# A float32 encoder trunk on one core: splits, products and weight sums of the adaLN parts placed elsewhere, and wo's early products in another order

## The chip, the core and the metric

The kernel runs on one core of one Trainium2 chip. The core has a matrix engine (TensorE, in the profile PE, with its weight loads as PEld), a vector engine (VectorE, DVE), a scalar engine (ScalarE, ACT), GpSimd (POOL), and SyncE (SP), which here issues most of the DMAs. Each engine works off its own list of instructions in order; semaphores hold an instruction until what it needs is there. The metric is the device time of one execution in microseconds. Before the change it is **1129.53 us**, the median of 3 runs (1127.41 to 1130.43).

## The reference

512 tokens of width 1024 go through two layers. Each has a token mixer (stick-breaking attention in layer 0, a gated token-mixing MLP in layer 1) and a SwiGLU network. Every one of these four sub-layers is wrapped like this:

```python
def ada_modulation(c, w, b):
    m = jax.nn.silu(c) @ w + b
    shift, scale, gate = jnp.split(m, 3, axis=-1)
    return shift[:, None, :], scale[:, None, :], gate[:, None, :]

def swiglu(h, w_gate, w_up, w_down):
    return (jax.nn.silu(h @ w_gate) * (h @ w_up)) @ w_down
...
    shift, scale, gate = ada_modulation(c, ffn_ada_w[i], ffn_ada_b[i])
    h = rms_norm(x, ffn_pre_g[i]) * (1.0 + scale) + shift
    y = swiglu(h, ffn_w_gate[i], ffn_w_up[i], ffn_w_down[i])
    x = x + gate * rms_norm(y, ffn_post_g[i])
```

The mixers have the same frame with their own weights. D_MODEL is 1024, D_FF 2816, everything is float32. What matters here: the adaLN vectors (shift, scale, gate) come from one row vector, silu(c), times a 1024 by 3072 matrix for each of the four sub-layers, 12 MB each.

## The kernel before

**Matmuls.** Tokens lie in four tiles of 128 (NT). A float32 matmul is made of three products of a short float format (`mm3`, L101): high by high, high by low, low by high. `split` (L109) makes the two parts of a value: the high one is a copy on ScalarE, the low one a subtraction on VectorE. In the profile wh and wl are the parts of a weight block, acch and accl those of a half adaLN sum, and as stands for both parts of an activation block. A result gathers in a PSUM bank of 128 by 512. There are six banks with the tag "b" and two with the tag "p" (`bank`, L50).

**Weights** are streamed: `wload` (L124) issues a load of 512 KB into one of two raw buffers, `wemit` (L134) splits it into one of six buffers, `wget` (L203) hands blocks out and stays three blocks ahead. All of these loads go through SP's queue, in the order in which they are written.

**adaLN parts** are made by the class `Bg` (L313), in small steps beside the main matmuls. G, A and B are the gate, the scale and the shift of a sub-layer; A1, B1, G2 and so on carry its number. For each part the eight row blocks of the matrix (rawada, 512 KB each, in two buffers of their own) are multiplied by silu(c) per partition and added to a 128 by 1024 accumulator on VectorE, one `ada_stt` (L306) a block. What remains is the sum over partitions. It is a product with a matrix of ones on TensorE: the accumulator is split in two halves of 512, and each half takes two matmuls (high, low) into a bank of tag "p", in the profile adaps. Then the bank is evacuated: B by a copy on ScalarE, A and G on VectorE, with a norm weight (pre_g or post_g, in the profile g, a load of 512 KB) multiplied in. The generator `run` (L338) yields after each sum, and before the change twice between split and product. `step` (L378) takes it on by so many yields.

**The output projection** `out_proj` (L493) loops over blocks k of its weights and within them over the token tiles; each gives 6 matmuls of 512 columns (two halves by three). For w_down of layer 0 (nk = 22, four of them held back as a tail) it also feeds two `Bg`s: `bg` with A1, B1, G2, two sums a step over the 12 steps k = 0 to 11, and then `bg2` with A2, B2 one sum a step. Token tile 0 gathers in the two "p" banks, which the adaLN products need too. So at `mid` = 13 the partial of tile 0 is copied out (yp), the products use the two banks, and tile 0 takes them again for the rest:

```python
            bg.step(steps)
            if bg2 is not None and mid is not None and k >= mid:
                bg2.step(1)
            if k + 1 == mid:
                yp = slot(F32, "yp")
                for hf in range(2):
                    act.activation(yp[:, hf, :], y[last][hf][:], AF.Copy)
                bg.step(99)
```

**The attention stage** has a generator of filler work (`filler`, L793) that a table of numbers deals out between the parts of a head pair. Its last items are the first four blocks (NEARLY = 4) of the projection wo for the token tiles 3 and 2; tile 3 gathers in the "p" banks, which the products of the last head pair's k and q have used before.

**Order.** In the attention stage all engines keep the order in which the code is written. In w_down and the gMLP stage the compiler's scheduler places instructions by their dependencies, so a step of `Bg` may come out some matmuls later than it is written. `blocks` (L170) makes the derived weight blocks of the SwiGLU stage, in the buffers f13, b21 and f24 (beside e, for silu); between the SwiGLU stages of the two layers these lie idle. `gmlp` (L1303) steps `bg2` on, through the remaining sums of A2 and B2 and their products.

## Time and profile before

| | us |
|---|---|
| runs: median (lowest, highest) | 1129.53 (1127.41, 1130.43) |
| the profiled execution | 1129.13 |
| its span in the trace | 1127.4 |

By stage, from the busy time of each engine in seven stretches of the span:

| stretch, us | stage | PE busy | DVE busy | ACT busy | DMA share |
|---|---|---|---|---|---|
| 0 to 75 | start, qkv begin | 66.42 | 55.98 | 46.44 | 0.80 |
| 75 to 229 | attention, wo | 152.27 of 154 | 123.44 | 100.90 | 0.50 |
| 229 to 505 | SwiGLU 0, gate and up | 276.00 of 276 | 233.86 | 154.56 | 0.44 |
| 505 to 640 | w_down 0 | 132.56 of 135 | 99.97 | 51.82 | 0.70 |
| 640 to 760 | gMLP | 120.00 of 120 | 73.96 | 48.62 | 0.47 |
| 760 to 1000 | SwiGLU 1, gate and up | 240.00 of 240 | 209.59 | 136.01 | 0.38 |
| 1000 to 1127.4 | w_down 1, end | 120.49 | 96.75 | 60.67 | 0.32 |

The granted TensorE clock is 0.99 to 1.00 in every stretch. The table is read by what is missing: TensorE is idle in the first stretch, in the last, and by 1.7 and 2.4 us in the two stretches in which the adaLN parts and wo's early products are made.

In a row of the profile L64 is the helper through which VectorE's and ScalarE's instructions pass, L90 the matmul in `mm`, L98 a transpose, L107 `load`; names are written out<-in without numbers.

### The profile page before, as it was taken

Reading aid. Unit: us, or ns where it says so; the run is one execution under the profiler, and the core shown is the slowest. Engines: PE = TensorE matmul, PEld = TensorE weight load, DVE = VectorE, ACT = ScalarE, POOL = GpSimd, SP = SyncE. Lnnn points to the kernel's source line nnn. Section 1 sums busy time; section 2 is a strip of 40 time slices with the busy share of each in tenths; the row PEclk is TensorE's granted clock in tenths of the full one; section 3 lists DMA queues with packets and bytes.
Section 4 is the critical chain, followed back from the end, with each engine's and each line's share of the span. In section 5 each row is a group of like instructions: output and inputs, shape, how many; then the busy total and the mean of one; then the engine's idle time right before and its main releaser. Section 6 shows DMA issues by size and latency. Waiting matters only on the chain.

```text
span 1127.4 us, 18149 instructions
## 1 busy us (share of the span) xinstructions
PE 1107.7 (98%) x7264; PEld 993.5 (88%) x7264; DVE 893.6 (79%) x1141; ACT 599.0 (53%) x971; POOL 39.7 (4%) x71
## 2 busy tenths in 40 slices
PE   7999999999999999999999999999999999999997
PEld 5788878779999999988878988989999999998895
DVE  7777888759988989687687774659988988788964
ACT  7746767646555555562234534437555555565541
POOL 0220111000000000010000000000000000000000
PEclk9999999999999999999999999999999999999999
DMA  9676445353344444378874583333244444223242
GB/s 363 228 229 164 146 145 164 124 187 131 95 131 150 149 137 129 93 231 262 285 259 158 186 281 89 99 131 131 76 150 149 130 133 133 76 86 105 91 168 75
DMA packets 51298, 176.09 MB, mean 156 GB/s; under 512 B 5643, under 2 KB 6155, under 8 KB 50318
## 3 DMA queue, kind: packets, MB, share of 16 engines
q1 hardware_dynamic: 45166, 153.95, 41.8%
q0 software_dynamic: 6048, 20.98, 5.9%
q8 instruction: 57, 0.93, 0.3%
q14 instruction: 27, 0.22, 0.1%
HBM read 164.43 MB, written 8.39 MB: 153 GB/s over the span
## 4 chain that ended last, share of the span: by engine, by line
PE 84%; DMA 7%; DVE 5%; issue 2%; ACT 1%; SPq 0%; POOL 0%; DVEq 0%; POOLq 0%; ACTq 0%
PE r L90 33%; PE y L90 12%; PE X L90 8%; PE v L90 7%; PE gu L90 6%; DMA rawada<-in_ada 5%; PE pqk L90 5%; PE u L90 4%; PE M L90 2%; PE z L90 1%; PE tw L98 1%; PE av L90 1%; DMA ada<-in_ada0w 1%; PE tp L98 1%; DMA raw<-in_wdown 1%
## 5 line engine op out<-in xcount | busy, mean ns | idle before, releaser
L64 ACT ACTIVATE wh<-raw 128x1024 fp32r<-128x1024 f32 (+1 forms) x112 | 116.8, 1050 | 139.6 <-PE y L90 41.2
L64 DVE TENSOR_TENSOR wl<-raw,wh 128x1024 fp32r<-128x1024 f32 (+1 forms) x112 | 135.0, 1211 | 65.8 <-ACT wh L64 65.5
L90 PE MATMUL r<-Sh,wh 128*128 128x256 f32 x608 | 170.6, 281 | 0.0
L90 PE MATMUL r<-Sl,wh 128*128 128x256 f32 x608 | 170.5, 280 | 0.0
L90 PE MATMUL r<-Sh,wl 128*128 128x256 f32 x608 | 170.3, 280 | 0.0
L90 PE MATMUL y<-wh,as 128*128 128x512 f32 x480 | 153.6, 396 | 0.2 <-DVE G L64 0.2
L64 DVE TENSOR_TENSOR wl<-f,wh 128x1024 fp32r<-128x1024 f32 x76 | 92.8, 1222 | 36.2 <-ACT wh L64 36.2
L64 ACT ACTIVATE wh<-f 128x1024 fp32r<-128x1024 f32 x76 | 80.6, 1061 | 68.4 <-PE r L90 65.1
L90 PEld LDWEIGHTS r<-Sh,wh 128*128 128x128 f32 x608 | 114.8, 189 | 0.2 <-ACT e L64 0.2
L90 PEld LDWEIGHTS r<-Sh,wl 128*128 128x128 f32 x608 | 114.7, 189 | 0.0
L90 PEld LDWEIGHTS r<-Sl,wh 128*128 128x128 f32 x608 | 114.7, 189 | 0.0
L90 PEld LDWEIGHTS y<-wh,as 128*128 128x128 f32 x480 | 90.1, 188 | 21.6 <-DVE G L64 0.7
L90 PE MATMUL y<-wl,as 128*128 128x512 f32 x240 | 94.8, 395 | 0.0
L90 PE MATMUL r<-hTh,wh 128*128 128x256 f32 x304 | 88.9, 293 | 0.0
L90 PE MATMUL r<-hTl,wh 128*128 128x256 f32 x304 | 85.1, 280 | 0.0
L90 PE MATMUL X<-wh,as 128*128 128x512 f32 (+1 forms) x288 | 84.6, 370 | 0.0
L90 PE MATMUL r<-hTh,wl 128*128 128x256 f32 x304 | 80.3, 280 | 0.0
L64 ACT ACTIVATE e<-r 128x256 f32<-128x256 f32 x114 | 43.3, 380 | 52.7 <-PE r L90 52.4
L90 PEld LDWEIGHTS r<-hTh,wh 128*128 128x128 f32 x304 | 57.3, 188 | 4.5 <-DVE gu L64 0.6
L90 PEld LDWEIGHTS X<-wh,as 128*128 128x128 f32 x288 | 52.5, 188 | 9.5
L90 PE MATMUL r<-hTh,b 128*128 128x256 f32 x304 | 60.8, 282 | 0.0
L64 ACT ACTIVATE wh<-rawx 128x1024 fp32r<-128x1024 f32 x38 | 40.3, 1062 | 36.8 <-PE r L90 31.1
(233 smaller groups left out, 2811.8 us busy)
## 6 DMA issues: line engine op xcount, KB each, us to landing
rawada<-in_ada SPq DMA_DIRECT2D x56, 512.0 KB, 5.0
raw<-in_wdown SPq DMA_DIRECT2D x44, 512.0 KB, 4.2
rawy<-in_wy SPq DMA_DIRECT2D x38, 512.0 KB, 3.7
rawx<-in_wx SPq DMA_DIRECT2D x38, 512.0 KB, 4.6
rawada<-in_ada POOLq DMA_DIRECT2D x24, 512.0 KB, 4.3
raw<-in_wqk SPq DMA_DIRECT2D x16, 512.0 KB, 3.8
ada<-in_ada0w SPq DMA_DIRECT2D x7, 1026.0 KB, 10.9
raw<-in_wgu SPq DMA_DIRECT2D x12, 512.0 KB, 3.6
```

The costliest lines, as they stand in the source:

```text
L64: b = f(*a, **k)
L90: b = nc.tensor.matmul(o, l, r, start=start, stop=stop, skip_group_check=True)
L98: last_tp[0] = nc.tensor.transpose(o, i, ident)
```

## The change

It has two parts.

1. In `filler` the loops over halves and blocks change places: half 0 of a token tile takes all four blocks of wo before half 1 begins.
2. `Bg` gets a flag `hold`, set for A1, B1, G2 in w_down of layer 0 and for A2, B2. With it, an accumulator is split right behind its last sum, into buffers that the SwiGLU's weight sums leave idle (`store`); the products need no split any more and come one half (two matmuls) a yield, so with two yields a step A, B and G take k = 12, 13 and 14. `out_proj` holds back tile 0's products of k = 13 and 14 (`put`) and does them at k = 15 together with those of k = 15; the sums of A2 begin at `mid + 2` instead of `mid`.

```diff
@@ class Bg
-        def __init__(self, *parts, slots=False, queue=nc.sync):
-            self.slots = slots
+        def __init__(self, *parts, slots=False, hold=False, queue=nc.sync):
+            self.slots, self.hold = slots, hold
...
         def run(self):
-            for name, at, s, part in self.parts:
+            for n, (name, at, s, part) in enumerate(self.parts):
...
                     ada_stt(acc, raw, k)
+                    if k == KD - 1 and self.hold:
+                        held[name, at] = self.store(n)
+                        for b, (h, l) in enumerate(zip(*held[name, at])):
+                            split(h, l, acc[:, b * 512 : (b + 1) * 512])
                     if not self.slots:
                         yield
...
                 for b in range(2):
                     c = slice(b * 512, (b + 1) * 512)
-                    h = adas.tile([P, 512], F32R, tag="acch", name=nm("acch"))
-                    l = adas.tile([P, 512], F32R, tag="accl", name=nm("accl"))
-                    split(h[:], l[:], acc[:, c])
-                    yield
-                    yield
+                    if self.hold:
+                        h, l = [t[b] for t in held[name, at]]
+                    else:
+                        h = adas.tile([P, 512], F32R, tag="acch", name=nm("acch"))[:]
+                        l = adas.tile([P, 512], F32R, tag="accl", name=nm("accl"))[:]
+                        split(h, l, acc[:, c])
+                        yield
+                        yield
                     ps = self.bank()
...
                         dve.tensor_tensor(acc[:, c], ps[:], g[:, c], ALU.mult)
+                    if self.hold:
+                        yield
+
+        def store(self, n):
+
+            fp = fwork["pool"]
+            if n == 0:
+                t = [fp.tile([P, 2, 512], F32R, tag="f13", name=nm("acc")) for _ in range(2)]
+                return [[x[:, b, :] for b in range(2)] for x in t]
+            if n == 1:
+                return [
+                    [fp.tile([P, 512], F32R, tag=f"b21{i}", name=nm("acc"))[:] for _ in range(2)]
+                    for i in range(2)
+                ]
+            t = fp.tile([P, 2, 512], F32R, tag="f24", bufs=1, name=nm("acc"))
+            return [
+                [t[:, b, :] for b in range(2)],
+                [
+                    fp.tile([P, 768], F32R, tag="e", name=nm("acc"))[:, :512] for _ in range(2)
+                ],
+            ]
@@ out_proj
+        put = []
         for k in range(nk - J):
             a = get_act(k)
             w = pre["w"][k] if k < npre else wget(wkey(k))
+            put.append((k, a, w))
             for tt in range(NT):
-                if k >= npre or tt not in pre["y"]:
+                if mid is not None and tt == last and k >= mid:
+                    if k >= mid + 2:
+                        for j in put:
+                            step(j[0], tt, *j[1:])
+                elif k >= npre or tt not in pre["y"]:
                     step(k, tt, a, w)
-            bg.step(steps)
-            if bg2 is not None and mid is not None and k >= mid:
+            if mid is None or k + 1 < mid or k >= mid + 2:
+                put = []
+            if bg2 is not None and mid is not None and k >= mid + 2:
                 bg2.step(1)
             if k + 1 == mid:
+                put = []
                 yp = slot(F32, "yp")
                 for hf in range(2):
                     act.activation(yp[:, hf, :], y[last][hf][:], AF.Copy)
-                bg.step(99)
+            bg.step(steps)
         bg.step(99)
@@ filler
-                for k, w in enumerate(early["w"]):
-                    for hf in range(2):
+                for hf in range(2):
+                    for k, w in enumerate(early["w"]):
@@ the calls
-    bg2 = Bg("A2", "B2")
+    bg2 = Bg("A2", "B2", hold=True)
     f0.run(
-        Bg("G1", slots=True), Bg("A1", "B1", "G2"), bg2, 2, hT2,
+        Bg("G1", slots=True), Bg("A1", "B1", "G2", hold=True), bg2, 2, hT2,
```

How the instructions move, at three places. In the rows below numbers behind a name tell buffers apart.

The first is TensorE in the attention stage, at the start of tile 3's early products: y_1806 and y_1810 are its halves 0 and 1, wh_1616/wl_1617 are the weights of k = 1, 1708/1709 of k = 2, 1802/1803 of k = 3 (the three rows of k = 0 stand ahead). A row with - is only in the kernel before, one with + only in the changed one:

```order
 L90 MATMUL y_1806<-wh_1616,o_1142 128x512
-L90 MATMUL y_1810<-wh_1616,o_1142 128x512
-L90 MATMUL y_1810<-wl_1617,o_1142 128x512
-L90 MATMUL y_1810<-wh_1616,o_1142 128x512
+L90 MATMUL y_1806<-wh_1708,o_1311 128x512
+L90 MATMUL y_1806<-wl_1709,o_1311 128x512
+L90 MATMUL y_1806<-wh_1708,o_1311 128x512
+L90 MATMUL y_1806<-wh_1802,o_1473 128x512
+L90 MATMUL y_1806<-wl_1803,o_1473 128x512
+L90 MATMUL y_1806<-wh_1802,o_1473 128x512
 L90 MATMUL z_532<-k_1770,q_1685 128x128
```

In the kernel before the 12 matmuls ahead of z take k = 0 and 1 for both halves, and now k = 0 to 3 for half 0 alone; half 1 opens its bank behind z.

The second place is the end of the sums of G2 in w_down of layer 0, on ScalarE and on SP. acc_5670 holds the high parts of G2's sum (G_5546), wh_5728 is the split of w_down's block 16, yp the copy of tile 0's partial. ScalarE in the changed kernel:

```order
L64 ACTIVATE wh_5682<-raw_5680 128x1024
L64 ACTIVATE acc_5670<-G_5546 128x512 x2
L64 ACTIVATE wh_5728<-raw_5726 128x1024
L64 ACTIVATE wh_5763<-raw_5761 128x1024
L64 ACTIVATE yp_5710<-y_5180 128x512
L64 ACTIVATE yp_5710<-y_5184 128x512
L64 ACTIVATE as_5723<-act_4044 128x512
```

SP in the changed kernel; raw_5798 is block 18 of w_down, g_5713 the norm weight for A1's evacuation, A_5842 the bias row of A2, and rawada are row blocks for sums:

```order
L107 DMA rawada_5847<-in_ada 128x1024
L107 DMA raw_5798<-in_wdown 128x1024
L107 DMA g_5713<-in_pre_g 128x1024
L107 DMA g_5785<-in_post_g 128x1024
L107 DMA A_5842<-in_adab 1x1024
L107 DMA raw_5853<-in_wdown 128x1024
```

SP in the kernel before, where g_5689 is the same norm weight:

```order
L107 DMA rawada_5493<-in_ada 128x1024
L107 DMA g_5689<-in_pre_g 128x1024
L107 DMA rawada_5496<-in_ada 128x1024
L107 DMA rawada_5535<-in_ada 128x1024
L107 DMA raw_5583<-in_wdown 128x1024
```

On ScalarE the split of G2 now stands ahead of the weight splits of blocks 16 and 17. On SP the load of g has gone from the midst of G2's row blocks to behind the load of block 18.

The third place is VectorE where G2 is evacuated. In the kernel before, with G_5532 for G2 and A_5779 for the accumulator of A2:

```order
L64 SCALAR_TENSOR_TENSOR A_5779<-rawada_5820,sc,A_5779 128x1024
L64 TENSOR_TENSOR G_5532<-adaps_5732,g_5726 128x512
L64 TENSOR_TENSOR accl_5737<-G_5532,acch_5736 128x512
L64 SCALAR_TENSOR_TENSOR A_5779<-rawada_5856,sc,A_5779 128x1024
L64 TENSOR_TENSOR G_5532<-adaps_5740,g_5726 128x512
```

In the changed kernel, with A_5212 for A1, G_5546 for G2 and A_5842 for A2:

```order
L64 SCALAR_TENSOR_TENSOR A_5212<-adaps_5715,g_5713 128x512
L64 SCALAR_TENSOR_TENSOR A_5212<-adaps_5719,g_5713 128x512
L64 TENSOR_TENSOR wl_5801<-raw_5798,wh_5800 128x1024
L64 SCALAR_TENSOR_TENSOR A_5842<-rawada_5845,sc,A_5842 128x1024
L64 TENSOR_TENSOR as_5943<-act_4798,as_5943 128x512
L64 SCALAR_TENSOR_TENSOR A_5842<-rawada_5847,sc,A_5842 128x1024
L64 TENSOR_TENSOR as_5946<-act_5049,as_5946 128x512
L64 TENSOR_TENSOR as_5949<-act_5049,as_5949 128x512
L64 SCALAR_TENSOR_TENSOR A_5842<-rawada_5883,sc,A_5842 128x1024
L64 SCALAR_TENSOR_TENSOR A_5842<-rawada_5919,sc,A_5842 128x1024
L64 TENSOR_TENSOR G_5546<-adaps_5787,g_5785 128x512
L64 TENSOR_TENSOR G_5546<-adaps_5791,g_5785 128x512
```

Before, one sum of A2 stands between the evacuations of G2's halves and one ahead of them; now four stand between A1's evacuations and G2's first, together with a weight split (wl_5801). Behind G2's first evacuation TensorE opens tile 0's bank again, in both kernels.

More of the change, by code (lines that the diff above doesn't have):

```diff
@@ L309, in ada_stt @@
         )
-    ada = {}
+    ada, held = {}, {}
     class Bg:
-        def __init__(self, *parts, slots=False, queue=nc.sync):
-            self.slots = slots
+        def __init__(self, *parts, slots=False, hold=False, queue=nc.sync):
+            self.slots, self.hold = slots, hold
             self.queue = queue
@@ L362, in run @@
                     c = slice(b * 512, (b + 1) * 512)
-                    h = adas.tile([P, 512], F32R, tag="acch", name=nm("acch"))
-                    l = adas.tile([P, 512], F32R, tag="accl", name=nm("accl"))
-                    split(h[:], l[:], acc[:, c])
-                    yield
-                    yield
+                    if self.hold:
[6 more added lines that the diff above has]
+                        yield
                     ps = self.bank()
-                    mm(ps[:], ones_r, h[:], True, False, last_tp[0])
-                    mm(ps[:], ones_r, l[:], False, True)
+                    mm(ps[:], ones_r, h, True, False, last_tp[0])
+                    mm(ps[:], ones_r, l, False, True)
                     if part == 0:
```

## The prediction, made before the changed kernel ran

> **What bounds the kernel now.** I read the page first, then the list of waits, TensorE's timeline at its waits, the chain, and the tile views of what is late.

> ```profile
> PE 1107.7 (98%) x7264; PEld 993.5 (88%) x7264; DVE 893.6 (79%) x1141; ACT 599.0 (53%) x971; POOL 39.7 (4%) x71
> ...
> PE adaps L90 <- ACT acch L64: 2.2, 1, 2.2
> PE y L90 <- DVE k L64: 1.7, 1, 1.7
> PE y L90 <- DVE G L64: 0.2, 1, 0.2
> ```

> TensorE (PE) is busy for 98% of the span, so a change that keeps its matmuls can only gain what PE now waits. Between 30 and 1110 us it has these three waits (total, times, longest). Part one of the change (wo's early products) stands at the second, part two (the adaLN sums in the first w_down projection) at the others. PE's timeline there:

> ```profile
> 563.79 0.39 PE L90 MATMUL adaps<-acch,ones 128*128 128x512 f32 x1
> ...
> 565.40 0.62 PE L90 MATMUL y<-wh,as 128*128 128x512 f32 x2
> 568.23 0.51 PE L90 MATMUL adaps<-acch,ones 128*128 128x512 f32 x1 [2.20 <-ACT acch L64]
> ...
> 580.85 0.50 PE L90 MATMUL y<-wh,as 128*128 128x512 f32 x1 [0.24 <-DVE G L64]
> ```

> In brackets: the idle time and what ended it. The most that can be gained is 1.73 + 2.20 + 0.24 = 4.2 us, 0.37% of the profiled execution's 1129.13 us (its span is 1127.4; the median of the runs shown, 1129.53, is 0.4 higher). A difference under 0.3% (3.4 us) can hardly be told from none. The first row also gives the pace: seven matmuls of 512 columns start between 563.79 and 565.40, 0.23 us each. The chain says why PE stood still:

> ```profile
> 560.38 6.11 DMA raw<-in_wdown
> ...
> 566.60 1.06 ACT wh L64
> 567.65 0.53 ACT acch L64
> ...
> 568.23 0.51 PE adaps L90
> ...
> 573.13 5.68 DMA rawada<-in_ada
> ...
> 578.90 1.28 DVE A L64
> 580.19 0.61 DVE G L64
> ...
> 580.85 19.17 PE y L90 x81
> ```

> The split of a sum (acch, on ScalarE, ACT) stood behind a weight split (wh) that waited for its load. Later G's evacuation on VectorE (DVE) stood behind a sum of A2 that waited for its load. The second is the pattern to watch: an in-order engine holds an evacuation that PE wants, behind an instruction that waits for a transfer.

> **Part one, wo's early products.** Token tile 3's half 0 now takes k = 0 to 3 before half 1 opens its bank.

> ```profile
> 198.81 2.33 DVE L64 TENSOR_TENSOR_SCAN ga<-ga,tri 128x512 f32<-128x512 f32 x2
> 200.03 0.48 PE L90 MATMUL y<-wh,o 128*128 128x512 f32 x1
> 200.94 1.06 ACT L64 ACTIVATE wh<-raw 128x1024 fp32r<-128x1024 f32 x1
> 201.16 1.39 DVE L64 TENSOR_TENSOR k<-pqk,k 64x512 fp32r<-64x512 f32 x2
> 202.58 0.69 DVE L64 TENSOR_TENSOR o<-av,o 128x512 fp32r<-128x512 f32 x1
> 202.70 0.47 PE L90 MATMUL y<-wh,o 128*128 128x512 f32 x1 [1.73 <-DVE k L64]
> 203.19 1.22 DVE L64 TENSOR_TENSOR wl<-raw,wh 128x1024 fp32r<-128x1024 f32 x1
> 204.88 0.22 PE L90 MATMUL z<-k,q 128*128 128x128 f32 x1
> ```

> Before, the fourth of these 12 matmuls waits until DVE has emptied the bank (k ends at 202.55). After, nine run from 200.03 to about 202.2, and the tenth needs k = 3's weights. Their high part is there (200.94 + 1.06 = 202.0). Their low part (wl) comes behind k and o on a DVE that has no gap from 198.81 on: 203.19 + 1.22 = 204.41. The eleventh so starts at about 204.5, the twelfth 0.34 later as the second one behind such a wait (200.03 to 200.34 would be 0.31), and z at 205.1 against 204.88. **One wait takes the other's place: +0.2 us** (bounds 0 and +0.4), not −1.73.

> **Part two, the sums in w_down 0.** Each sum is split as soon as it is complete, the six products run two a step at k = 12, 13, 14, and the fresh banks of token tile 0 open at k = 15 instead of 13. The acch wait of 2.20 goes. Six ACT and six DVE splits are moved, not added; the sums of A2 start two steps later, and with them their loads on SP's queue. What is late next is G's evacuation, by a chain that the rows price one by one:

> ```profile
> 557.93 1.28 DVE L64 SCALAR_TENSOR_TENSOR G<-rawada,sc,G 128x1024 f32<-128x1024 f32 x1 [1.48 <-DMA rawada<-in_ada]
> 559.13 1.22 DVE L64 TENSOR_TENSOR wl<-raw,wh 128x1024 fp32r<-128x1024 f32 x1
> ...
> 560.38 0.33 SPq L107 DMA_DIRECT2D raw<-in_wdown  x1
> 560.76 0.42 SPq L107 DMA_DIRECT2D g<-in_post_g  x1
> 560.82 1.07 ACT L64 ACTIVATE yp<-y 128x512 f32<-128x512 f32 x2
> ...
> 566.06 0.68 DVE L64 SCALAR_TENSOR_TENSOR A<-adaps,g 128x512 f32<-128x512 f32 x1
> 573.62 1.29 DVE L64 TENSOR_TENSOR as<-act,as 128x512 fp32r<-128x512 f32 x2
> ...
>   DMA rawada<-in_ada: 15.6, 15
> ...
> DMA to landing us min/median/max: 3.6/4.6/5.7
> ...
> DMA to landing us min/median/max: 4.2/5.2/7.4
> ...
> DMA to landing us min/median/max: 7.4/7.4/7.4
> ```

> The last four rows are of the tile views from 520 on: DVE's wait for rawada (15.6 us in 15 waits: the sums are paced by their loads), and the time from issue to landing of rawada, of w_down's raw and of g.

> 1. The last sum of G ends at 559.2. Three inserted pairs of low splits (0.6 each) stand between sums that wait for loads anyway; I let half a microsecond through: 559.8 (bounds 558.9 and 561.0).
> 2. G's split on ACT, two halves, 1.07 like the pair yp: 560.9. It stands ahead of the wh of w_down's block 16, which ran at 559.86 before.
> 3. That wh 1.06: 561.9. Its wl 1.22: 563.1. This frees a raw buffer, and only now SP can issue block 18's raw, with the load of **g** (pre_g, for A's evacuation) queued behind it, 0.38 later: 563.5. (Behind that stand the other g, A2's bias and the next raw.)
> 4. g lands. The one g on record took 7.4, raw's median is 5.2, the shortest transfer of this size 3.6. I take 6.3, midway between raw's median and the g: 569.8 (bounds 3.6 and 7.4).
> 5. A's two evacuations, 1.29: 571.1. Only behind them come a wl (1.1 net of overlap: 572.2), the first two sums of A2 with an "as" of 0.6 between (1.2 + 0.6 + 1.2): 575.2.
> 6. The two sums free the buffers of two more loads of A2, and both sums that use those stand before G's evacuation on DVE. The second is issued at 575.2. I take the 5.68 that the chain shows for the same load at the same place (bounds 3.6 and 5.7): 580.9.
> 7. That sum 1.28, G's evacuation 0.6: 582.8. PE opens the bank at 582.9.

> PE gets there early. The new order has 54 matmuls between the first product (563.79) and this one: 563.79 + 54 × 0.235 = 576.5, with 0.235 from the 81 matmuls in 19.17 us. So PE loses some 6.4 us in all, the greater part, about 5, in one wait on G. Waits before it (for yp's bank, for A's evacuation) are swallowed: the bank opens at 582.9 whether PE waits once or thrice. Before, PE resumes at 580.85 with the 62nd matmul; after, this place in the count is seven further on, at 582.9 + 0.34 + 6 × 0.235 = 584.65. **+3.8 us**; all behind it is the same number of matmuls, and PE has no wait to give it back to.

> With the bounds: all loads at 3.6 and step 1 unchanged end the chain 5.4 earlier, at 577.5, and the step at −1.6. With 561.0 and a g of 7.4 the step is +5.8 to +6.

> The rest of the move I cost at nothing beside this. The deferred products are the same in number. They hold the weights of blocks 13 and 14 two steps longer, so the loads of the last blocks (19 to 21) come later, but PE wants those only in the tail, after 580.85 + 19.17 = 600, some 20 us behind A2's first sums; without that cover each late load would cost its own 4 to 5 us. POOL's clearing of A2's accumulator and its bias load move along and are short of the path by step 4's wait. In the gMLP stage the products of A2 and B2 follow at once, without the two empty steps:

> ```profile
> 667.00 2.61 DVE L64 SCALAR_TENSOR_TENSOR B<-rawada,sc,B 128x1024 f32<-128x1024 f32 x2 [1.02 <-DMA rawada<-in_ada]
> ...
> 671.54 0.40 PE L90 MATMUL adaps<-acch,ones 128*128 128x512 f32 x1
> ```

> The sums end at 669.6 and the first product of B2 is due some 16 matmuls behind the 671.54, at 675.3; A2's evacuation, behind one wh and one wl, is through at about 673.7. I take 0 (bound +1).

> Sum: 1129.13 + 0.2 + 3.8 = **1133.1 us**.

> [...]

> **Rivals.** (a) *The loads are fast, and nothing changes.* The decisive point is the sum of the two loads in steps 4 and 6: at 12.0 − 3.8 = 8.2 us or less (3.6 + 4.6, for one) the change is not slower. For it: 3.6 and 4.6 are on record, and the new order moves A2's loads away. Against it: g, at its old place in this queue, took 7.4, and rawada in the chain 5.68. Time 1127.7 to 1131, the middle 1129.5; 0.17.

> (b) *The wait costs PE its clock too.* No mid-kernel wait of before exceeds 2.4 us; this one is about 5. At the kernel's start, after idle time, matmuls run slow:

> ```profile
> 2.92 3.78 PE L90 MATMUL sc<-pack,sc 128*128 128x128 f32 x16 [2.92 <-ACT sc L64]
> ...
> 9.04 3.32 PE L98 MATMUL tp<-pack,x 128*128 128x128 f32 x20 [0.25 <-DVE x L64]
> ...
> 192.39 1.03 PE L98 MATMUL tw<-pack,ga 128*128 128x128 f32 x8
> ```

> 16 of 128 columns take 3.78 (0.22 each, by their starts), 8 of 128 later take 1.03 with the tail of the last (0.11 each): half pace. The 20 from 9.04 take 3.32, so some nine of them are slow, until about 11: at most 8.1 us of half pace since 2.92, so at most 4.1 lost. With half of that or all of it the time is 1135.1 to 1137.2. Against it: the waits of 1.73 and 2.20 are followed by full pace at once. 0.22. [...]

> (c) *The change does what it says*, and the three waits go with nothing in their place: 1129.13 − 4.2 = 1124.9. It needs wl of k = 3 two microseconds earlier, and a G that no load of A2 holds; the order speaks against both. 0.04.

> **How the numbers follow.** Forecast 0.57, (a) 0.17, (b) 0.22, (c) 0.04. Slower by over 0.3% (above 1132.9): a little over half of the forecast's chance and all but little of (b), together 0.56. Faster by over 0.3% (below 1126.1): 0.04. Within: 0.40. The range leaves out (c), the lower half of (a) and the upper third of (b), together 0.19: 1129.4 to 1136.6.

> **What would show it.** PE's timeline at 202.4 to 204.5 has a wait of about 2 us, named wl, where k stood. At 576 to 583 it has waits that sum to 6 us, the longest on DVE's G, and the acch wait is gone. DVE idles for g until about 570 and for rawada until about 581. If the matmuls behind that wait start 0.43 apart for a while, (b) is right. The forecast is wrong if g or the last rawada lands in under 4.5 us, or if A's evacuation does not stand behind g; then PE opens the bank before 580.

## The result and the profile after

The changed kernel takes **1134.3 us** (median of 6 runs, 1130.09 to 1135.81) against 1129.32 before: a ratio of 1.0038, 95% interval 1.0022 to 1.0055. It is slower by 0.38%, or 4.3 us by the ratio. The profiled execution took 1132.64 us, with a span of 1130.9 against 1127.4.

The page of the changed kernel, busy time of each engine, and the list of what TensorE waited for (total, times, longest):

```profile
PE 1110.6 (98%) x7264; PEld 996.0 (88%) x7264; DVE 893.3 (79%) x1141; ACT 598.4 (53%) x971; POOL 39.8 (4%) x71
...
PE y L90 <- DVE G L64: 2.9, 1, 2.9
PE y L90 <- DVE wl L64: 1.9, 1, 1.9
PE r L90 <- DVE gu L64: 0.3, 1, 0.3
```

Both parts did what the diff says: the waits on k, on acch and the small one on G are gone. In their place stand a wait on wl at wo's early products and one on G in w_down. In sum the waits are little longer: 5.1 us against 4.1. The larger share is in the first row. PE's busy time has grown by 2.9 us (1107.7 to 1110.6) with the same 7264 instructions. The timeline of PE shows where, first at wo's early products and then in w_down:

```profile
204.44 0.50 PE L90 MATMUL y<-wl,o 128*128 128x512 f32 x1 [1.87 <-DVE wl L64]
...
205.01 0.22 PE L90 MATMUL z<-k,q 128*128 128x128 f32 x1
...
206.27 0.63 PE L90 MATMUL y<-wh,o 128*128 128x512 f32 x1
206.70 0.63 PE L90 MATMUL y<-wl,o 128*128 128x512 f32 x1
...
577.97 0.40 PE L90 MATMUL y<-wh,as 128*128 128x512 f32 x1
581.22 0.62 PE L90 MATMUL y<-wh,as 128*128 128x512 f32 x1 [2.85 <-DVE G L64]
581.64 0.63 PE L90 MATMUL y<-wl,as 128*128 128x512 f32 x1
582.07 1.05 PE L90 MATMUL y<-wh,as 128*128 128x512 f32 x2
...
585.21 0.39 PE L90 MATMUL y<-wl,as 128*128 128x512 f32 x1
585.44 0.63 PE L90 MATMUL y<-wh,as 128*128 128x512 f32 x2
```

Matmuls of 512 columns start 0.43 apart at 206.27 and 206.70, and again from 581.22 on, where 0.23 is the usual pace (585.21 to 585.44). TensorE ran at **half pace** for 3.4 us at each of the two waits, and each stretch cost about 1.5 us, by an estimate from the 2.9 above. The granted TensorE clock (the column behind POOL busy) says the same when it is asked for narrow stretches of the changed kernel:

```profile
core 0: us, PE busy (x) PEld busy (x) DVE busy (x) ACT busy (x) POOL busy (x), PEclk, DMA share, GB/s
202.57:205.98 3.41, 1.54 (x10) 1.45 (x11) 3.41 (x4) 1.07 (x2) 0.00 (x0) 1.00 0.82 272
205.98:209.40 3.42, 3.42 (x11) 2.73 (x11) 2.48 (x3) 1.00 (x2) 0.00 (x0) 0.50 0.80 273
581.45:584.86 3.41, 3.41 (x9) 2.61 (x9) 1.60 (x2) 0.80 (x1) 0.00 (x0) 0.50 0.71 221
```

In the profile of before there is no half pace in mid-kernel: its granted clock is 1.00 in each stretch of 40 us from 30 to 1110. The chain of the changed kernel, from the sums to the reopened bank:

```profile
563.14 1.06 ACT wh L64
564.20 0.97 ACT yp L64 x2
565.18 0.52 ACT as L64
...
565.73 3.13 DVE as L64 x6
...
569.35 0.99 DVE A L64 x2
...
570.54 1.21 DVE wl L64
571.76 1.21 DVE A L64
...
572.98 4.89 DMA rawada<-in_ada
...
577.96 1.30 DVE A L64
...
580.48 0.70 DVE G L64
...
581.22 23.99 PE y L90 x95
```

The second half of it is the one forecast: evacuation of A, a weight split, sums of A2, a load for the next sums, these sums, and only then G's evacuation.

### The profile page after: what moved, and what is told of

The parts are those of the page before. It is cut to its first block, busy times and chain, and to the rows that moved or that the text cites. A ratio compares the mean times of both kernels' runs of the same rounds, so it can differ in the third digit from the quotient of the medians.

```text
span 1130.9 us, 18147 instructions
## 1 busy us (share of the span) xinstructions
PE 1110.6 (98%) x7264; PEld 996.0 (88%) x7264; DVE 893.3 (79%) x1141; ACT 598.4 (53%) x971; POOL 39.8 (4%) x71
## 4 chain that ended last, share of the span: by engine, by line
PE 82%; DVE 7%; DMA 7%; issue 2%; ACT 1%; SPq 0%; POOL 0%; DVEq 0%; ACTq 0%; POOLq 0%
PE r L90 31%; PE y L90 12%; PE X L90 8%; PE v L90 7%; PE gu L90 6%; PE pqk L90 5%; PE u L90 4%; DMA rawada<-in_ada 4%; PE M L90 2%; DVE wl L64 2%; PE z L90 1%; DMA raw<-in_wdown 1%; PE tw L98 1%; DMA ada<-in_ada0w 1%; PE av L90 1%
## 5 line engine op out<-in xcount | busy, mean ns | idle before, releaser
L64 DVE TENSOR_TENSOR wl<-raw,wh 128x1024 fp32r<-128x1024 f32 (+1 forms) x112 | 135.0, 1211 | 67.6 <-ACT wh L64 67.3
L64 ACT ACTIVATE wh<-raw 128x1024 fp32r<-128x1024 f32 (+1 forms) x112 | 116.8, 1050 | 120.8 <-PE y L90 34.7
L90 PE MATMUL r<-Sh,wh 128*128 128x256 f32 x608 | 170.5, 280 | 0.0
L90 PE MATMUL r<-Sl,wh 128*128 128x256 f32 x608 | 170.5, 280 | 0.0
L90 PE MATMUL r<-Sh,wl 128*128 128x256 f32 x608 | 170.3, 280 | 0.0
L90 PE MATMUL y<-wh,as 128*128 128x512 f32 x480 | 154.1, 398 | 2.9 <-DVE G L64 2.9
L64 DVE TENSOR_TENSOR wl<-f,wh 128x1024 fp32r<-128x1024 f32 x76 | 92.8, 1221 | 36.1 <-ACT wh L64 36.1
L64 ACT ACTIVATE wh<-f 128x1024 fp32r<-128x1024 f32 x76 | 80.6, 1061 | 68.8 <-PE r L90 65.3
L90 PEld LDWEIGHTS r<-Sh,wh 128*128 128x128 f32 x608 | 114.8, 189 | 0.2 <-ACT e L64 0.2
L90 PEld LDWEIGHTS r<-Sh,wl 128*128 128x128 f32 x608 | 114.7, 189 | 0.0
L90 PEld LDWEIGHTS r<-Sl,wh 128*128 128x128 f32 x608 | 114.7, 189 | 0.0
L90 PEld LDWEIGHTS y<-wh,as 128*128 128x128 f32 x480 | 90.9, 190 | 24.3 <-DVE G L64 3.3
L90 PE MATMUL y<-wl,as 128*128 128x512 f32 x240 | 95.5, 398 | 0.0
L90 PE MATMUL r<-hTh,wh 128*128 128x256 f32 x304 | 88.8, 293 | 0.3 <-DVE gu L64 0.3
L90 PE MATMUL r<-hTl,wh 128*128 128x256 f32 x304 | 85.1, 280 | 0.0
L90 PE MATMUL X<-wh,as 128*128 128x512 f32 (+1 forms) x288 | 84.7, 370 | 0.0
L90 PE MATMUL r<-hTh,wl 128*128 128x256 f32 x304 | 80.2, 280 | 0.0
L64 ACT ACTIVATE e<-r 128x256 f32<-128x256 f32 x114 | 43.5, 381 | 52.7 <-PE r L90 52.4
L90 PEld LDWEIGHTS r<-hTh,wh 128*128 128x128 f32 x304 | 57.2, 188 | 4.9 <-DVE gu L64 1.3
L90 PEld LDWEIGHTS X<-wh,as 128*128 128x128 f32 x288 | 52.5, 188 | 9.6
L90 PE MATMUL r<-hTh,b 128*128 128x256 f32 x304 | 60.8, 282 | 0.0
L64 ACT ACTIVATE wh<-rawx 128x1024 fp32r<-128x1024 f32 x38 | 40.3, 1061 | 36.8 <-PE r L90 31.0
```

The source lines that it names most:

```text
L64: b = f(*a, **k)
L90: b = nc.tensor.matmul(o, l, r, start=start, stop=stop, skip_group_check=True)
```

## The experiments

Two theories were put against each other. **Theory 1:** the change swaps waits for waits of the same length, and the surplus is half pace behind them. **Theory 2, the forecast's:** the chain over A2's sums makes TensorE wait longer, and the pace plays no part. Times are medians; ratios are to the kernel before on the same chip, whose median was 1129.88 (35 runs) beside the first four, 1129.52 (29) beside the next four and 1130.52 (23) beside the last three.

| run | kernel | us | ratio, 95% interval |
|---|---|---|---|
| e1 | part one alone | 1132.98 | 1.0014 (0.9999 to 1.0029) |
| e2 | part two alone | 1133.24 | 1.0028 (1.0012 to 1.0043) |
| e3 | changed, pads of zeros in both waits | 1132.98 | 1.0022 (1.0010 to 1.0033) |
| e4 | changed, A2's sums behind G's evacuation | 1128.19 | 0.9984 (0.9970 to 0.9998) |
| e5 | changed, once more | 1134.68 | 1.0033 (1.0019 to 1.0048) |
| e6 | as e3, tile 1's matmuls ahead of the pads | 1130.78 | 1.0014 (1.0003 to 1.0024) |
| e7 | before, another order of wo's early products | 1127.46 | 0.9987 (0.9975 to 0.9998) |
| e8 | e4 and e7 together | 1126.46 | 0.9967 (0.9955 to 0.9979) |
| e9 | before, with pads | 1131.15 | 1.0012 (0.9996 to 1.0027) |
| e10 | e8 once more | 1125.73 | 0.9951 (0.9931 to 0.9970) |
| e11 | part two alone, A2's sums behind G's evacuation | 1128.30 | 0.9974 (0.9963 to 0.9986) |

### e1 and e2: each part alone

e1 is the kernel before with the two loops exchanged, e2 the changed kernel with the loops as before:

```diff
-                for k, w in enumerate(early["w"]):
-                    for hf in range(2):
+                for hf in range(2):
+                    for k, w in enumerate(early["w"]):
```

> Part one alone on the kernel before. Theory 1 (the change swaps waits for waits of the same length, and its surplus is TensorE at half pace after them, as the profile of the changed kernel shows at 206.3 to 209.0 and at 581.2 to 584.6): the wait of 1.73 us on k is replaced by one of about 1.87 on wl, z starts 0.1 to 0.2 us later, and in some executions a stretch of half pace follows that loses about 1.6 us, so the median lies 0 to 1.8 us above the kernel before. Theory 2 (the forecast: the waits themselves are longer and the pace plays no part): +0.2 us, with no more spread than before.

> Part two alone: the changed kernel with the loops of wo's early products as before. Theory 1: TensorE waits 2.5 to 3.5 us on G at about 579, in place of 2.20 + 0.24 before, and a half-pace stretch behind it loses 1.6: +1.5 to +3 us. Theory 2: the wait on G is about 5 us long, with full pace behind it: +3.8 us. If the chain that ends in G keeps its absolute time, TensorE comes to it 1.7 us earlier than in the changed kernel and the wait is that much longer, so the sum is near that of the changed kernel (+3.5) even without part one.

e1 is 1.6 us slower by the ratio (−0.1 to +3.3), which is not clear of zero. Its runs fall into two groups: 7 of 12 lie above 1132 us, against 7 of 35 for the kernel before. The granted clock on record for each run goes with this: its mean over the run is 0.993 to 0.996 in those seven, and 0.996 to 0.999 in the five others. VectorE's last sum ahead of wo's early products in its profile, the waits of TensorE, and what follows the first:

```profile
197.81 1.28 DVE L64 SCALAR_TENSOR_TENSOR B<-rawada,sc,B 128x1024 f32<-128x1024 f32 x1 [1.68 <-DMA rawada<-in_ada]
...
PE adaps L90 <- ACT acch L64: 2.8, 1, 2.8
PE y L90 <- DVE wl L64: 2.6, 1, 2.6
...
207.81 0.63 PE L90 MATMUL y<-wh,o 128*128 128x512 f32 x1
208.24 0.63 PE L90 MATMUL y<-wl,o 128*128 128x512 f32 x1
```

The wait on wl was longer than forecast here, 2.63 us: VectorE had come late, by a sum of B that waited 1.68 for its load ahead of the scan (0.90 in the profile of before). Half pace follows, 0.43 from start to start, and here it lasts longer: at least from 205.25 to 210.38, 5.1 us against 3.4. So part one, meant for a wait of 1.73, swaps it for one that is as long or longer.

e2 gives +0.28%, the larger part of the change's +0.38% (+0.33% when it was run again, e5). G's evacuation starts at 580.0 there and at 580.5 in the changed kernel, although TensorE came to its first product 1.3 us earlier (564.40 against 565.73). In these two profiles the chain keeps its time, and what TensorE loses ahead of it is swallowed by the wait. The times do not show this: the parts sum to +0.42%, and with the intervals that is not told apart from the whole.

### e3 and e6: TensorE kept busy in the waits

Matmuls with a stationary matrix of zeros add nothing to a bank but occupy TensorE (22 of them take 5.30 us in e3). The two places in e3:

```diff
...
+                        if (tt, hf, k) == (3, 0, 3):
+                            for _ in range(8):
+                                mm(y[0][:], zeros_r, early["w"][0][0][:, 0, c], False, False)
...
+                        if k == mid + 2:
+                            for _ in range(22):
+                                mm(y[3][1][:], zeros_r, put[0][2][0][:, 0, 0:512], False, False)
```

> The changed kernel with matmuls that add zeros to a bank (8 ahead of k = 3 in tile 3's half 0, 22 ahead of tile 0's new banks in w_down), so that TensorE is busy while it waits; at 0.233 us they take 1.9 and 5.1 us, about what the waits take with part one's half pace gone. Theory 1: the half-pace stretches go (-3.2 us in the profile), what is left is the exchange of waits, and pads that outlast the wait cost up to 1 us: 1129.5 to 1131.5, with a small spread. Theory 2: the waits set the time and the pads change nothing: 1133 to 1135.

In e3 the longest wait in mid-kernel is 0.3 us and the matmuls behind the second pads start 0.23 to 0.24 apart (from 581.23 on), and yet the time is that of e2 (+0.22% against +0.28%). The timeline of e3 shows a flaw of the experiment: the six matmuls of tile 1 that fill the wait in the changed kernel (1.4 us) had slipped behind the pads. e6 puts them ahead, with 14 pads.

> As the first padded kernel, but with tile 1's six matmuls of k = 15 ahead of the pads, where the changed kernel has them, and 14 pads in place of 22. Theory 2: G's evacuation starts at 580 to 581 as in the first padded kernel, and with full pace behind it the later part of the kernel is 1.4 us earlier than there: 1131 to 1132.3, which is 1.3 to 2.5 above the kernel before, all of it the chain. Theory 1: without half pace the kernel is level with the one before, 1129 to 1130.3.

PE in e6 at the second wait:

```profile
576.72 0.39 PE L90 MATMUL y<-wh,as 128*128 128x512 f32 x1
576.95 3.44 PE L90 MATMUL y<-wh,zeros 128*128 128x512 f32 x14
580.22 0.39 PE L90 MATMUL y<-wh,as 128*128 128x512 f32 x1
580.45 0.39 PE L90 MATMUL y<-wl,as 128*128 128x512 f32 x1
```

VectorE in e6, where G is evacuated:

```profile
579.13 1.28 DVE L64 TENSOR_TENSOR G<-adaps,g 128x512 f32<-128x512 f32 x2
```

The pads fill the wait, the pace behind it is full (0.23 from 580.22 to 580.45), and the median falls to 1130.78, 3.5 us under the changed kernel (3.9 under e5). Medians exaggerate this, since the runs of the changed kernel lie in groups: by the ratios to the kernel before, +0.14% against +0.38% and +0.33%, it is 2.1 to 2.7 us. e6 stays above the kernel before, by 0.14% or 1.6 us (0.3 to 2.7). That is about the chain's share without half pace. G's evacuation started earlier than the 580 to 581 that was expected, and the first of its two halves was through by 579.8, so that the pads outlast the wait by about 0.4 us in this profile. So both theories hold, each for a part.

### e4: the sums of A2 out of the way

```diff
-                    ada_stt(acc, raw, k)
+                    b = ada_stt(acc, raw, k)
+                    if k == 0 and (name, at) == ("A", 2):
+                        order(b, held["G"])
...
-                        dve.tensor_tensor(acc[:, c], ps[:], g[:, c], ALU.mult)
+                        held["G"] = dve.tensor_tensor(acc[:, c], ps[:], g[:, c], ALU.mult)
```

> The changed kernel with the first sum of A2 ordered behind G's second evacuation on VectorE, nothing else. If the sums of A2 (and the two loads that they wait for) hold G's evacuation, as the chain says, the evacuation follows its product at about 577, the wait of 2.85 us on G goes and the half-pace stretch with it: about 4.5 us less than the changed kernel, 1129 to 1130.5. If G's own chain (split, weight split, load of the norm weights) is what is late, the wait stays and the time is 1133 to 1135.

VectorE in e4:

```profile
569.14 1.28 DVE L64 SCALAR_TENSOR_TENSOR A<-adaps,g 128x512 f32<-128x512 f32 x2
570.34 1.22 DVE L64 TENSOR_TENSOR wl<-raw,wh 128x1024 fp32r<-128x1024 f32 x1
...
575.92 1.29 DVE L64 TENSOR_TENSOR G<-adaps,g 128x512 f32<-128x512 f32 x2 [2.56 <-PE adaps L90]
577.12 2.60 DVE L64 SCALAR_TENSOR_TENSOR A<-rawada,sc,A 128x1024 f32<-128x1024 f32 x2
```

G's evacuation now waits for its product, not for a load, and starts at 575.92 instead of 580.48. TensorE has no wait left in w_down, and the kernel takes 1128.19: 6 us less than the changed kernel (4.5 expected), and faster than the kernel before by 0.16% (0.02 to 0.30). A2's sums, which come later, make nothing else late: the longest wait of TensorE behind them is 0.2 us. This is the proof of the chain: one dependency on VectorE's order, no work taken away.

### e5: the changed kernel again

> The changed kernel once more, for a second profile and more runs. If the chain over A2's sums sets the time (theory 2), G's evacuation again starts at 580 to 581.5 whatever TensorE did before, and the runs lie at 1132 to 1135. If half pace after waits is most of the surplus (theory 1), runs without it come down to the level of the kernel before, 1129 to 1130, in about a quarter of the cases.

The result repeats: +0.33% (0.19 to 0.48). Three of 12 runs lie under 1131 (1129.19 to 1130.91), the share that theory 1 expects; seven lie at 1134.66 or above. That the three are the runs without half pace is not shown: their mean granted clocks are 0.996, 0.998 and 0.995, and the profiled run, with two stretches of half pace, has 0.996. The profiled one took 1136.00; its chain and its waits:

```profile
567.72 2.63 DVE as L64 x5
...
576.77 5.67 DMA rawada<-in_ada
...
584.48 20.70 PE y L90 x81
...
PE y L90 <- DVE G L64: 4.5, 1, 4.5
PE y L90 <- DVE wl L64: 3.1, 1, 3.1
```

G's evacuation started at 583.74, outside the 580 to 581.5 that was expected: the last load took 5.67 us (at most 4.4 in the first profile) and the sums of G had ended later, at 561.1. Half pace followed both waits (starts 0.42 apart at 208.30 and 208.72, and at 585.88 and 586.30). As far as two profiles show it, the wide spread of this kernel has these two sources, the loads in the chain and the pace.

### e7, e8, e10: both waits mended

e7 is the kernel before with this order for tile 3, which puts the first product of half 1 fourth, after nine matmuls that need nothing late:

```diff
+                first = [(0, 0), (0, 1), (0, 2), (1, 0), (0, 3), (1, 1), (1, 2), (1, 3)]
...
```

> The kernel before, with half 0 of tile 3 taking k = 0, 1, 2 and then half 1 its k = 0 ahead of the z matmuls. If the bank of half 1 is what is late there (free at 202.6 to 203.0) the nine matmuls end at 202.2 and TensorE waits 0.3 to 0.9 us in place of 1.73: 1128 to 1129.5 and fewer runs above 1132. If another thing is late right behind it (the weights of k = 3, the z matmuls' operands), a wait of the same sum appears there and the time stays at 1129.9.

PE in e7 at wo's early products, and then at the old wait on acch:

```profile
203.04 0.47 PE L90 MATMUL y<-wh,o 128*128 128x512 f32 x1 [0.49 <-DVE k L64]
...
203.81 0.22 PE L90 MATMUL z<-k,q 128*128 128x128 f32 x1
...
567.58 0.50 PE L90 MATMUL adaps<-acch,ones 128*128 128x512 f32 x1 [2.42 <-ACT acch L64]
...
570.08 0.63 PE L90 MATMUL y<-wl,as 128*128 128x512 f32 x1
570.51 0.63 PE L90 MATMUL adaps<-acch,ones 128*128 128x512 f32 x1
```

The wait is 0.49 us, z starts at 203.81 instead of 204.88, and the kernel gains 0.13% (0.02 to 0.25). The second wait is still there, and here half pace follows it: in the profile of before a wait at the same place, 2.20, did not bring it (granted clock 1.00 from 563 to 590).

> The changed kernel with A2's sums behind G's evacuation, as in the fourth run, and with the order of wo's early products of the run above. If both waits are gone, no wait above 1 us is left in mid-kernel and no half pace either: 1125 to 1127 with little spread, faster than the kernel before by 3 to 4.5 us.

> The eighth kernel again, since few of its runs were undisturbed: 1125.5 to 1127 and all runs within 2 us, if no wait is left that can bring half pace.

The two cures together give 1126.46 and 1125.73, faster than before by 0.33% and 0.49%, with all ten runs between 1125.06 and 1127.21. The longest wait on TensorE is 1.1 us in e8 and 0.9 in e10, and the mean granted clock of both profiled executions is 0.998, as in the profile of before. e10's gain is 5.5 us by the ratio (3.4 to 7.8), and the three waits of the kernel before sum to little over 4; what half pace costs the kernel before in some of its runs can be the rest, but the interval holds 4.2, the most that the prediction allowed, too. This is the version to keep.

### e9 and e11

> The kernel before, with matmuls that add zeros so that TensorE is busy in its two waits: 7 ahead of half 1's first product among wo's early ones (1.6 us for a wait of 1.73), 9 ahead of tile 3 at k = 12 of w_down (2.1 us for a wait of 2.20). If half pace behind these waits costs the kernel before something too, its runs above 1131 go and the median falls to 1128.3 to 1129.2. If half pace is a matter of the changed kernel alone, the median stays at 1129.4 to 1130 and so does the spread.

e9 does not answer its question. The time is unchanged (1.0012, 0.9996 to 1.0027), and 6 of 12 runs still lie above 1131. In its profile (1133.97, mean granted clock 0.998) the matmuls behind the first pads run at full pace, 0.23 apart from 203.72 to 205.36, but TensorE comes to the first product at 567.04 in place of 563.79, and it waits 1.5 us on acch and another 1.5 on accl, which was no wait before. Whether the pads moved the sums so was not tested. How much half pace costs the kernel before stays open. The granted clocks of its runs hint at it: beside the first four experiments the 10 runs with a mean of 0.998 or 0.999 take 1128.9 us on the average, the 11 with 0.996 or less 1131.0; beside the others it is 1129.0 against 1130.7 and 1129.6 against 1132.0. These are runs laid side by side, not a test, and they do not tell where in the kernel the clock was low.

> Part two alone, with A2's sums behind G's evacuation and wo's early products as in the kernel before. The wait of 1.73 on k stays, the 2.20 and 0.24 go with nothing in their place: 1126.9 to 1128.3, with a second group of runs 1.5 to 2 us higher where half pace follows the wait on k. If it is no faster than the kernel before, the sums that now come later make something else late.

e11 gains 0.26% without part one. Its one long wait is on k, 2.29 us in the profile, with half pace behind it (starts 0.43 apart at 205.40 and 205.83). So part two is worth having once A2's sums are behind G, and part one, in its form in the change, adds nothing to it that can be seen (e4, with both: −0.16%).

## Why the prediction was right

The forecast was 1133.1 us, the measured time is 1134.3. The sign, the place and the kind of wait were right, but two errors in opposite directions meet in the sum: the wait on G was put too long in the first profile, and the pace behind the waits was put at nothing. That the number came out so close is in part luck. In the first profile TensorE's waits grew by 1.0 us, where the forecast had some 4, and its busy time, by the pace, by 2.9.

**Part one, +0.2.** The wait on wl came as worked out (204.44 against 204.5, z at 205.01 against 205.1), so its own term is +0.13. What failed is that nothing was put down for the pace behind it, about 1.5 us in this profile. Alone part one costs 1.6 us by the ratio, and that is not clear of zero.

**Part two, +3.8.** e4 shows that the chain is the cause. Its size without half pace is 1.6 us by e6 (0.3 to 2.7). By the working of the forecast, in which a bank opened at 582.9 is +3.8, the bank's opening gives +2.1 in the first profile, +1.6 in e2 and +5.4 in e5, all at full pace. By its steps in the first profile:

| step | forecast | first profile | e5 |
|---|---|---|---|
| 1, last sum of G ends | 559.8 | 560.5 | 561.1 |
| 5, second sum of A2 ends | 575.2 | 574.8 | 576.7 |
| 6, last load takes | 5.68 | at most 4.4 | 5.67 |
| 7, PE opens the bank | 582.9 | 581.2 | 584.5 |

Step 4 was the wrong link. The load of g did not hold A's evacuation: it was issued at 564.3 and VectorE did not wait for it. Six low parts of activations (as) stood ahead of the evacuation until 569.4. The time came out nearly the same, 570.6 against 571.1 for the end of A's evacuations, by another road. Step 6 is the term that was mis-sized in the first profile: the second sum starts at 579.2 right behind the first, so its load, issued at 574.8, took 4.4 us at most. The chain there goes over the load ahead of it, 4.89 us, and G came 1.7 us earlier than forecast. e5 shows the other end of the same spread. The forecast took the longest of the loads for the rule. Two of its own signs of being wrong so came true in the first profile, the last load in under 4.5 us and A's evacuation not behind g; that the bank still opened behind 580 goes with the six low parts, which stood in g's place and which the working did not have. Its upper bound is a slip of 0.1: 561.0 and a g of 7.4 add 1.2 and 1.1 to 3.8, which is 6.1.

**Waits in between.** The forecast had 6.4 us of waiting, 5 of them on G. It was 2.85, 3.1 (e2) and 4.5 (e5). In the first profile TensorE came to the bank 1.7 us later than worked out, by part one's wait and half pace, and this shortened the wait without moving its end.

**Rival (b), half pace, at 0.22,** is what made up the rest, and it was held too unlikely: it followed the wait on G in the first profile and in e5 (starts 0.42 to 0.43 apart from 581.22 and from 585.88). Its price of 2.0 to 4.1 us was too high, since a stretch lost about 1.5. The argument against it, that the waits of 1.73 and 2.20 were followed by full pace at once, was true of one execution only. In e7 a wait of 2.42 at the place of the 2.20 is followed by half pace. Waits of the old length can bring it, so the new wait on wl could too; it was priced for the long wait alone.

**Rival (a)** had its decisive point in the sum of two loads; only the second counted. **Rival (c)**, at 1124.9, is what e10 comes within 0.8 us of, beside a kernel before that took 1130.52 there: with a G that no load of A2 holds, as it was said to need, and with another order of products where it asked for an earlier wl. The terms put at nothing (the deferred products, the gMLP stage) were nothing: no wait of TensorE over 0.3 us appears there in the first profile.

## What to carry to other kernels

When splits or sums are moved on an in-order engine, look at what then stands ahead of the evacuation that the matrix engine waits for: an accumulation that waits for a load belongs behind it, and one ordering edge (e4) gave back more than the whole change had cost. A wait on the matrix engine should be priced with the pace behind it, here about 1.5 us for each stretch of 3.4 us at half the clock, and not from one profile. And where one buffer is late, look what else in the same stretch comes from the same late engine before the order is changed: k and wl came from the same queue, and only work that needed neither (e7) shortened the wait.

## What the runs showed of the hardware

| run | wait on | us | starts behind it | apart |
|---|---|---|---|---|
| before | k | 1.73 | 203.00, 203.24 | 0.24 |
| changed, first profile | wl | 1.87 | 206.27, 206.70 | 0.43 |
| e4 | wl | 2.17 | 206.82, 207.06 | 0.24 |
| before | acch | 2.20 | 568.57, 568.80 | 0.23 |
| e11 | k | 2.29 | 205.40, 205.83 | 0.43 |
| e7 | acch | 2.42 | 570.08, 570.51 | 0.43 |
| e1 | wl | 2.63 | 207.81, 208.24 | 0.43 |
| e1 | acch | 2.82 | 573.37, 573.80 | 0.43 |
| changed, first profile | G | 2.85 | 581.64, 582.07 | 0.43 |
| e5 | wl | 3.06 | 208.30, 208.72 | 0.42 |
| e5 | G | 4.51 | 585.88, 586.30 | 0.42 |

The 1.87 us with half pace behind them are fewer than 2.17 and 2.20, with full pace behind them; from 2.29 us on, half pace followed each of the seven. It need not come at once: in the first profile the wait of 1.87 ends at 204.44, and the granted clock falls to 0.50 at 205.98. Both waits there lie in the 3.41 us ahead of their half pace (202.57 to 205.98 with PE busy for 1.54 us, 578.04 to 581.45 with 0.56, granted clock 1.00 in both), and the ends of the two half-pace stretches, 209.40 and 584.86, are 375.46 us apart, 110 times 3.413. What besides the length tells the 1.87 from the 2.17 and the 2.20 was not shown.

A half-pace stretch is easily overlooked. The profile page's row of granted clock, in slices of 28 us, reads 9 throughout for the changed kernel; only the starts of the matmuls, or the granted clock of a stretch as narrow as the ones above, show it.
